# A causal convolution of four taps, moved from multiply-adds on VectorE to accumulating float32 matmuls on TensorE, in a hybrid decoder layer

## The chip, the cores and the metric

The kernel runs on one core of a Trainium2 chip. The metric is the device time of one execution in microseconds (us); lower is better. The kernel before took 1670.52 us, the median of three runs (1668.51 to 1672.82). The names of the engines are those of the profile: PE is TensorE's matmuls, PEld its weight loads, DVE is VectorE, ACT is ScalarE, POOL is GpSimd, and SP issues most of the transfers.

## The reference

One decoder layer for 1024 tokens of 1024 channels, everything in float32. A mixer (a gated delta rule of four heads of 128 channels, beside an S5 state space model of 512 channels) is followed by cross-attention to 256 memory tokens and by a SwiGLU. The part that the change touches is the way from the in-projection to the heads:

```python
def _causal_dwconv(x, w):                       # w: 4 taps for each channel
    return lax.conv_general_dilated(
        x, w[:, None, :], window_strides=(1,), padding=((CONV_WIDTH - 1, 0),),
        dimension_numbers=("NWC", "WIO", "NWC"), feature_group_count=x.shape[-1])

proj = xn @ w_in                                # xn = RMSNorm(x)
qkv = silu(_causal_dwconv(proj[..., OFF_Q:OFF_Z], conv_w))
q, k, v = three times 512 columns of qkv, as 4 heads of 128
...
mn = _rmsnorm(mem, norm_mem_g)
k = (mn @ w_xk).reshape(bsz, N_MEM, X_HEADS, X_HEAD_DIM)
v = (mn @ w_xv).reshape(bsz, N_MEM, X_HEADS, X_HEAD_DIM)
```

So each output of the convolution at token t is w0 p(t−3) + w1 p(t−2) + w2 p(t−1) + w3 p(t), channel by channel, with zeros ahead of the first token.

## The kernel before

Activations lie channel-major: 128 channels on the partitions, tokens along the free axis, in two halves of HT = 512 tokens (NT = 1024). Products that need float32 accuracy are made by `mm3` (L77 to L81): each operand is split into a high and a low part of a shorter format (fp32r), and three matmuls, high x high, low x high and high x low, accumulate in PSUM. A weight tile (`weight`) is loaded into `wraw` (two buffers), ACT copies its high part (L62, `whi`), and POOL or DVE subtracts for the low part (L63, `wlo`). A few small products are plain float32 matmuls.

The in-projection of q, k and v is twelve tiles of 128 channels, `in_tile(n)` for n = 0 to 11, twice 24 matmuls of 512 columns each. For each half DVE multiplies the PSUM tile by the row of reciprocal norms into `pre` (L477), which has four columns ahead of its tokens. Three of these are zeroed (L479, first half) or copied from the end of the first half (L481, second half). ACT then writes the first tap's product (L485), DVE adds the other three with three multiply-adds (L487), and ACT applies Silu in place (L488). `pre` has three buffers, in the pool `cv`.

For each head in turn the program makes its k and q tiles, the decays and products of keys (`dn_a`: L591 turns the keys token-major, L608 multiplies keys by keys, L626 queries by keys), its v tile, the token-major values (`dn_v`, L646) and the inverse of the chunks' triangles (`dn_b`, ending at L718). After the four heads eight chunks follow one another (`dn_seq`, L747 to L772), with the output norm and gate of each (`dn_tail`; its split is L65 and L66). In parallel the S5 part and its gate (`glu`, L902 and L904) run. Then come the operands of the output projection (`out_acts`, from L935) and the folding of memory keys into query weights (`fold_k`).

The memory tokens are normalised in `mem_prep`, and `mem_proj` makes their keys and values in 16 tiles (24 matmuls of 256 columns each). Each tile is copied by ACT from PSUM to a staging tile `mst` (L837) of the permanent pool `cp`, with one buffer, and stored to DRAM (`memD`). Later `mem_load` reads the keys and values back, into `kst` tiles of the pool `kv`.

PSUM has eight banks of 512 float32 columns. `mm` tiles come from the pool `pm` (three banks); `aux` tiles at this place come from `p5`, which has one bank.

The program is written in the order above, but a scheduler reorders the instructions of each engine by a model of times, within what buffers and data allow. Each engine, and SP's queue of transfers, then runs its instructions in that fixed order. A pool occupies its space from where it is opened to where it is closed: a pool that is opened in the space of a closed one gives its tiles only when the last users of the closed one are done. The pool `kv` is opened on the right side after `seq.close()`, which gives up the buffers of the delta rule.

Of the kernel before, what the change touches and what calls it, by code (L numbers as in the profile page):

```python
# [28 lines left out]
# columns of the packed constants: identity, upper triangle, diagonals and masks of 16-blocks  # L29
# [16 lines left out]
class Kernel:  # L46
# [12 lines left out]
    def split(self, src, hi, lo, scale=None, eng=None):  # L59
        """hi + lo = src * scale exactly, each with few enough bits for one pass of the tensor engine."""  # L60
        if scale is None:
            self.a.activation(out=hi, in_=src, func=AF.Copy)  # L62
            return (eng or self.v).tensor_tensor(out=lo, in0=src, in1=hi.bitcast(F32), op=ALU.subtract)  # L63
        else:
            self.a.activation(out=hi, in_=src, func=AF.Copy, scale=scale)  # L65
            self.v.scalar_tensor_tensor(out=lo, in0=src, scalar=scale, in1=hi.bitcast(F32), op0=ALU.mult, op1=ALU.subtract)  # L66

    def weight(self, src, n, m, eng=None):
        """src: DRAM [128, n, m] -> (hi, lo) [128, n, m]."""
        raw = self.wp.tile([P, n, m], F32, name="wraw", bufs=2)  # L70
        self.load(raw, src)
        hi = self.wp.tile([P, n, m], F32R, name="whi")
        lo = self.wp.tile([P, n, m], F32R, name="wlo")
        self.split(raw, hi, lo, None, eng)
        return hi, lo
# [24 lines left out]
    def exact_exp(self, out, x, n, r, w):  # L100
        """exp(x) to float32 accuracy, 0 below the normal range; n, r, w: scratch."""
# [14 lines left out]
    def colsum(self, ps, srcs):  # L116
        """ps[:, 64 i] = sums over the partitions of srcs[i] [128, 128]; -> view [128, n]."""
        for i, xs in enumerate(srcs):
            for j, x in enumerate(xs):
                self.lastc = self.te.matmul(ps[:, 64 * i:64 * i + 64], x, self.ones, start=(j == 0), stop=(j == len(xs) - 1))  # L120
        return ps[:, 0:64 * len(srcs)].rearrange("p (t n) -> p t n", n=64)[:, :, 0]

    def rstd(self, acc, nt, name, psum=None):
        """acc [128 ch, nt*128]: squares summed over channel tiles -> rstd [128 tok, nt]."""
# [10 lines left out]
    def rowbc(self, rs, nt, out, psum=None):  # L135
        """rs [128 tok, nt] -> out [128, nt*128], every row the same."""
# [13 lines left out]
    def s5_setup(self, tp):  # L150
# [24 lines left out]
        # cos and sin: quadrant reduction and series  # L175
# [35 lines left out]
        # a^p, p = 0..8  # L211
# [11 lines left out]
        # (a - 1) / (a_re + i a_im)  # L223
# [15 lines left out]
        # a^p co, as rows [re|im][p][pair (e s)]  # L239
# [10 lines left out]
        # discretised input matrices, block diagonal over the pair  # L250
# [13 lines left out]
        # unit phasors of a^(8 (n + 1))  # L264
# [23 lines left out]
        # impulse responses behind seven zero blocks  # L288
# [9 lines left out]
    def s5_pre(self, S, m, sp):  # L298
        """Matrices of eight groups (four pairs) for chunks of 8 tokens."""
# [8 lines left out]
        # (re, -im) of a^p c  # L308
# [18 lines left out]
        # impulse responses within a chunk  # L327
# [10 lines left out]
        # input matrices, rows (7 - j, c)  # L338
# [11 lines left out]
    def s5_toeplitz(self, S):  # L350
        """TT[(7 - j', c'), g, (j, c)] = response at lag j - j' of c to c'."""
# [3 lines left out]
    def s5_in(self, b, sp):  # L355
        """Inputs of the states of four groups at the chunks."""
# [18 lines left out]
    def s5_out(self, b, sp, M, U4, Tt, Pv):  # L375
        """States by a real scan in rotated axes, and the outputs."""
# [44 lines left out]
    def x_prep(self, h, cv, first=None):  # L421
        """Split gain * x for a token half; statistics for its RMSNorm."""
# [28 lines left out]
    def proj_tile(self, src, xh, xl, w=None, ps=None):  # L451
        """One 128-column tile of a projection for a token half, channel-major in PSUM."""
# [6 lines left out]
    def in_tile(self, n, cv, w=None, px=None, stats=False):  # L459
        """A tile of the in-projection, both halves; n: 0..11 q|k|v through the causal convolution, 12..15 u."""  # L460
# [3 lines left out]
        last = None  # L464
        for h in range(2):
# [4 lines left out]
            if n >= 12:  # L470
# [4 lines left out]
                continue  # L475
            pre = cv.tile([P, 4 + HT], F32, name="pre", bufs=3)
            v.tensor_tensor(out=pre[:, 4:], in0=ps, in1=rb, op=ALU.mult)  # L477
            if h == 0:
                v.memset(pre[:, 1:4], 0.0)  # L479
            else:  # L480
                v.tensor_copy(out=pre[:, 1:4], in_=last[:, HT + 1:HT + 4])  # L481
            last = pre
            cw = lambda i: self.convw[:, n, i:i + 1]
            acc = out[:, h * HT:(h + 1) * HT]
            self.a.activation(out=acc, in_=pre[:, 1:1 + HT], func=AF.Copy, scale=cw(0))  # L485
            for i in (1, 2, 3):
                v.scalar_tensor_tensor(out=acc, in0=pre[:, 1 + i:1 + i + HT], scalar=cw(i), in1=acc, op0=ALU.mult, op1=ALU.add)  # L487
            self.a.activation(out=acc, in_=acc, func=AF.Silu)  # L488
# [6 lines left out]
    def zab(self, cv):  # L495
        """z, a, b token-major: two blocks of 260 columns."""
        ab = cv.tile([P, 8, 8], F32, name="ab", bufs=1)
        for blk in (1, 0):
            ws = [self.weight(self.I["w_z"][blk, q], 4, 260) for q in range(2)]
            for c in range(8):  # L500
# [12 lines left out]
                zt = cv.tile([P, 260], F32, name="zt", bufs=2)  # L513
# [7 lines left out]
    def gates(self, ab, cv):  # L521
        """g = -exp(a_log) softplus(a + dt_bias), beta = sigmoid(b), and the cumulated g of each chunk."""
# [5 lines left out]
        # softplus(x) = max(x, 0) + log1p(exp(-|x|)); log1p(e) = 2 atanh(e / (2 + e))  # L528
# [33 lines left out]
    def dn_a(self, hd, q, k, dp, dx):  # L562
        """A head in eight chunks of 128 tokens: decays, products of keys and queries."""
# [12 lines left out]
        # decays  # L576
# [11 lines left out]
        # keys token-major  # L588
# [16 lines left out]
        # -L, strictly lower  # L605
# [7 lines left out]
        # its diagonal 16-blocks, every row on all 16 partitions of its block  # L613
# [9 lines left out]
        # queries against keys [s, c], s <= c  # L623
# [7 lines left out]
        # eps of the output norm, scaled by the norm of the query  # L631
# [9 lines left out]
    def dn_v(self, hd, vT, b1, dp):  # L641
        """Values token-major."""
# [8 lines left out]
    def dn_b(self, hd, L, R, dp):  # L651
        """The inverse of each chunk's triangle."""
# [10 lines left out]
        # N = (I + L)^-T: 16-blocks by substitution  # L663
# [12 lines left out]
        # doubled to 32, 64 and 128; M = N^T; only every second block of columns changes  # L676
# [46 lines left out]
    def slot(self, name):  # L723
        """The next of the buffers of a name in the space that the heads have left."""
# [4 lines left out]
    def dn_seq(self, c, dq):  # L729
        """The state across chunks, and the outputs of a chunk."""  # L730
# [44 lines left out]
    def dn_tail(self, c, po, dq, xs):  # L775
        """Norm and gate of a chunk's outputs, channel-major and split."""
# [22 lines left out]
    def mem_prep(self, cv):  # L799
        """RMSNorm of the memory tokens, split."""  # L800
        T = lambda n, i: self.tmp.tile([P, HT], F32, name=n, bufs=i)
        two = lambda t: t.rearrange("p (k t) -> p k t", k=2)
        raws = [T(n, 2) for n in ("res", "res", "fsg")] + [cv.tile([P, 4 + HT], F32, name="pre", bufs=3)[:, 4:]]
# [24 lines left out]
    def mem_proj(self, mem, w, dst):  # L828
        """Keys or values of the memory, channel-major."""
        mh, ml = mem  # L830
        for m in range(KD):
# [4 lines left out]
            t = self.cp.tile([P, NMEM], F32, name="mst")  # L836
# [11 lines left out]
    def fold_k(self, kv, K, m):  # L848
        """Query weights against the keys of each head: scores = x AD."""
# [11 lines left out]
    def fold_v(self, kv, V, hd, c):  # L861
        """Values of a head against the rows of the output weights."""
# [47 lines left out]
    def resid(self, w, order, xs, accs):  # L910
        """hT += w^T x for (tile, half) in order; squares summed on the way."""
# [10 lines left out]
    def out_acts(self, xs, tp):  # L922
        """Right sides of the seven products of the output projection."""
# [7 lines left out]
        def diff(x, y, k, name):  # L931
            """x - y of two operands in two parts."""
# [20 lines left out]
    def out_pair(self, mp, X, accs):  # L953
        """hT = x + w_out^T (outputs of the mixer) for two tiles and both halves, by seven products."""
# [63 lines left out]
    def scores(self, c, xs, rs, qp, between):  # L1018
        """Softmax of two heads for a half. The rows go without the factor of the RMSNorm: the softmax scale carries it."""
# [29 lines left out]
    def probs(self, p, pT, c, n):  # L1049
        """Probabilities of a head with a tile of the memory on the partitions, split."""  # L1050
# [20 lines left out]
    def ffn_prep2(self, acc, x0, xp, kx, T4):  # L1071
        """Right sides of the seven products, from the normalised rows of both halves."""
# [50 lines left out]
    def raw_pair(self, f, xp, gp):  # L1123
        """Gate and up columns of two tiles."""
# [8 lines left out]
    def ff_pair(self, f, raws, X, xp, gp, order, prep=None):  # L1133
        """Gate and up of two tiles and both halves, 2 x 2 blocks by seven products (Winograd's form of Strassen's)."""
# [25 lines left out]
        def add(u, o, x, y):  # L1160
            """have[o] = have[x] + have[y]; outputs are (tile, half)."""
# [54 lines left out]
    def down_acts(self, c, raw=None):  # L1216
        """Right sides of a chunk of four rows of the down projection, from DRAM: products 1, 2, 3 and 7, and the sums of the others."""
# [47 lines left out]
    def down_weights(self, c, mp, pool, n=2):  # L1265
        """Left sides of the seven products for two output tiles."""
# [17 lines left out]
    def down_products(self, c, mp, X, W):  # L1284
        """Seven products; those that enter several outputs gather in Q."""
# [24 lines left out]
    def out_rows(self, m, o):  # L1310
        """Output tile m for a token range within a half."""
# [3 lines left out]
    def down_last(self):  # L1315
        """Operands of the last two rows of the down projection."""
# [16 lines left out]
    def ff_down(self, m, o, acts, ws):  # L1333
        """The last two rows of the down projection into output tile m, for a token range."""
# [6 lines left out]
    def final(self, o, rs):  # L1341
        """Last RMSNorm of a token range."""
# [36 lines left out]
    def emit(self, ctx):  # L1379
# [73 lines left out]
        with psum("ps6", 1) as self.p6, psum("pds", 1) as self.ps, psum("pdo", 2) as self.po:  # L1453
# [19 lines left out]
            self.mem_proj(mem, "w_xk", self.memD[0])  # L1473
            self.mem_proj(mem, "w_xv", self.memD[1])
# [114 lines left out]
def _layout(x, mem, norm_mix_g, w_in, conv_w, dn_a_log, dn_dt_bias, dn_norm_g,  # L1589
# [11 lines left out]
    # channels of the S5 part: within a tile of eight groups, (channel, group)  # L1601
# [46 lines left out]
```

## Time and profile before

| | |
|---|---|
| median of three runs | 1670.52 us (1668.51 to 1672.82) |
| span of the profiled execution | 1669.7 us, 20638 instructions |
| busy ACT, POOL | 646.7 us (39%), 703.0 us (42%) |
| mean granted TensorE clock | 0.935 of full speed |
| bytes moved | 208.63 MB, 125 GB/s on the mean |
| last head's key products (L608) | at 370.3 us |
| last `pre` multiply (L477) and last Silu (L488) start | 378.9 and 388.9 us |
| staging copies of the memory (L837) | 16, from 392.9 to 578.8 us |

The profile is of one execution; times in it count from its first instruction. "Busy" is the time in which an engine ran an instruction. Matmuls are pipelined, so their records overlap; the price of one is read from the distance between the starts of neighbours. A wait is written as the waiting engine, tile and line, then "<-" and what released it.

### The profile page before, as it was taken

To read this page: it belongs to the slowest core of one execution; us is meant where nothing else is said; L and a number is where in the kernel's file an instruction comes from. 1 tells how busy PE (TensorE), PEld (TensorE's weight loads), DVE (VectorE), ACT (ScalarE), POOL (GpSimd) and SP (SyncE) were. 2 spreads that over 40 slices of the span, in tenths; PEclk is the share of its full clock that TensorE was granted. 3 is DMA by queue.
4 is the path that set the end of the run, shared out by engine and by line. 5 is a ranking of instruction groups with operands and counts; after the bars stand their busy time and mean duration, and the time that the engine had idled before them with its cause. 6 is when DMAs were issued, how large, how long until landed. Compare 5 with 4: busy or idle time off the path is not lost. (4 is left out here: it accounts for less than half of the span.)

```text
span 1669.7 us, 20638 instructions
## 1 busy us (share of the span) xinstructions
PE 1496.9 (90%) x7302; PEld 1245.7 (75%) x7302; DVE 1262.7 (76%) x2176; ACT 646.7 (39%) x1164; POOL 703.0 (42%) x507
## 2 busy tenths in 40 slices
PE   6887978988878988999999889999999997889985
PEld 4776767877878876878888668888888885677764
DVE  8968987976689898875547895555555559999995
ACT  5222443342345653454533333333333334433322
POOL 6074432313444566610011554333333357556554
PEclk8998989989688989999999889999999999999997
DMA  6256534345686453235424212322222134233202
GB/s 215 79 163 199 175 92 115 94 123 177 222 297 234 145 171 120 89 127 175 153 89 151 88 57 85 105 89 88 88 77 82 51 122 181 89 101 101 89 0 101
DMA packets 123894, 208.63 MB, mean 125 GB/s; under 512 B 10224, under 2 KB 69520, under 8 KB 121232
## 3 DMA queue, kind: packets, MB, share of 16 engines
q1 hardware_dynamic: 123792, 207.33, 38.6%
q8 instruction: 57, 0.93, 0.2%
q14 instruction: 45, 0.37, 0.1%
HBM read 151.34 MB, written 58.05 MB: 125 GB/s over the span
## 5 line engine op out<-in xcount | busy, mean ns | idle before, releaser
L62 ACT ACTIVATE whi<-wraw 128x1024 fp32r<-128x1024 f32 (+2 forms) x176 | 154.0, 881 | 284.4 <-PE aux L81 77.6
L63 POOL TENSOR_TENSOR wlo<-wraw,whi 128x1024 fp32r<-128x1024 f32 x48 | 121.6, 2533 | 203.5 <-ACT whi L62 191.0
L79 PE MATMUL mm<-AH,whi 128*128 128x512 f32 x436 | 175.6, 403 | 1.1 <-ACT whi L62 1.1
L81 PE MATMUL mm<-AH,wlo 128*128 128x512 f32 x420 | 168.3, 401 | 0.0
L80 PE MATMUL mm<-AL,whi 128*128 128x512 f32 x396 | 158.4, 400 | 0.0
L147 POOL TENSOR_TENSOR acc<-acc,sq 128x512 f32<-128x512 f32 (+1 forms) x41 | 55.4, 1351 | 213.0 <-ACT sq L146 212.2
L63 DVE TENSOR_TENSOR wlo<-wraw,whi 128x1024 fp32r<-128x1024 f32 (+2 forms) x76 | 95.8, 1263 | 32.1 <-ACT whi L62 32.1
L1174 POOL TENSOR_TENSOR sg<-sg,ca 128x512 f32<-128x512 f32 x44 | 67.0, 1522 | 113.0 <-DVE sg L1167 82.0
L79 PEld LDWEIGHTS mm<-AH,whi 128*128 128x128 f32 x436 | 83.6, 192 | 19.6 <-ACT whi L62 1.8
L80 PE MATMUL aux<-AL,whi 128*128 128x512 f32 x228 | 92.3, 405 | 6.0 <-POOL AL L63 3.7
L81 PEld LDWEIGHTS mm<-AH,wlo 128*128 128x128 f32 x420 | 80.4, 191 | 18.2 <-issue 0.4
L80 PEld LDWEIGHTS mm<-AL,whi 128*128 128x128 f32 x396 | 76.4, 193 | 16.5
L487 DVE SCALAR_TENSOR_TENSOR it<-pre,convw,it 128x512 f32<-128x512 f32 x72 | 74.8, 1039 | 6.5 <-ACT it L485 5.7
L79 PE MATMUL aux<-AH,whi 128*128 128x512 f32 x188 | 75.1, 400 | 3.3 <-ACT whi L62 2.6
L62 ACT ACTIVATE wlo<-graw 128x512 fp32r<-128x512 f32 x66 | 41.6, 630 | 79.5 <-PE aux L81 57.1
L81 PE MATMUL aux<-AH,wlo 128*128 128x512 f32 x172 | 69.3, 403 | 0.0
L81 PE MATMUL aux<-AH,whi 128*128 128x512 f32 x148 | 58.6, 396 | 0.0
L80 PEld LDWEIGHTS aux<-AL,whi 128*128 128x128 f32 x228 | 44.1, 193 | 17.7 <-POOL AL L63 5.3
L79 PE MATMUL aux<-AH,wlo 128*128 128x512 f32 x132 | 53.9, 408 | 3.2 <-DVE sq L1167 3.2
L80 PE MATMUL aux<-AL,wlo 128*128 128x512 f32 x132 | 53.7, 406 | 0.0
L79 PEld LDWEIGHTS aux<-AH,whi 128*128 128x128 f32 x188 | 36.0, 192 | 12.5 <-ACT whi L62 2.8
L1172 ACT ACTIVATE ca<-ca 128x512 f32<-128x512 f32 x44 | 27.8, 632 | 35.6 <-DVE ca L1167 34.7
(699 smaller groups left out, 4745.3 us busy)
## 6 DMA issues: line engine op xcount, KB each, us to landing
graw<-in_w_up SPq DMA_DIRECT2D x22, 512.0 KB
actD<-sg SPq DMA_DIRECT2D x44, 256.0 KB
wraw<-in_w_down SPq DMA_DIRECT2D x20, 512.0 KB
wraw<-in_w_in SPq DMA_DIRECT2D x16, 512.0 KB
d_X<-XD SPq DMA_DIRECT2D x8, 1024.0 KB
wraw<-AD SPq DMA_DIRECT2D x16, 512.0 KB
wraw<-VD SPq DMA_DIRECT2D x16, 512.0 KB
wraw<-in_w_gate SPq DMA_DIRECT2D x12, 512.0 KB
```

The costliest lines, as they stand in the source:

```text
L62: self.a.activation(out=hi, in_=src, func=AF.Copy)
L63: return (eng or self.v).tensor_tensor(out=lo, in0=src, in1=hi.bitcast(F32), op=ALU.subtract)
L79: mm(ps, wh, xh, start=first, stop=False)
L80: mm(ps, wh, xl, start=False, stop=False)
L81: mm(ps, wl, xh, start=False, stop=last)
L147: eng.tensor_tensor(out=acc, in0=acc, in1=tmp, op=ALU.add)
L487: v.scalar_tensor_tensor(out=acc, in0=pre[:, 1 + i:1 + i + HT], scalar=cw(i), in1=acc, op0=ALU.mult, op1=ALU.add)
L1172: A.activation(out=r, in_=r, func=AF.Silu)
L1174: g.tensor_tensor(out=r, in0=r, in1=sg[o], op=ALU.mult)
```

## The change

For the q, k and v tiles, ACT first makes a tile `diag` of four 128 x 128 matrices, the identity scaled by each tap's 128 values (four copies per tile). `pre` now holds both halves behind its four columns and has two buffers; POOL zeroes the three columns once. The multiply by the norms stays on DVE. When both halves are there, each half is convolved by four plain float32 matmuls that accumulate in one bank of `p5`, with `diag` as weights and `pre`, shifted by a token each, as the moving side; ACT applies Silu from PSUM into `it`.

Other tiles move as well. `zt` in `zab` takes slots of `pre`, one raw tile of `mem_prep` becomes an `it` slot, and `mem_proj` copies into `kst` (four buffers, pool `kv`) in place of `mst`. Comments are taken out, so that lines from about L490 on stand two lower.

```diff
     def in_tile(self, n, cv, w=None, px=None, stats=False):
...
-        last = None
+        if n < 12:
+            diag = cv.tile([P, 4, P], F32, name="diag")
+            for i in range(4):
+                self.a.activation(out=diag[:, i], in_=self.ident, func=AF.Copy, scale=self.convw[:, n, i:i + 1])
+            pre = cv.tile([P, 4 + NT], F32, name="pre", bufs=2)
+            self.g.memset(pre[:, 1:4], 0.0)
         for h in range(2):
...
-                continue
-            pre = cv.tile([P, 4 + HT], F32, name="pre", bufs=3)
-            v.tensor_tensor(out=pre[:, 4:], in0=ps, in1=rb, op=ALU.mult)
-            if h == 0:
-                v.memset(pre[:, 1:4], 0.0)
             else:
-                v.tensor_copy(out=pre[:, 1:4], in_=last[:, HT + 1:HT + 4])
-            last = pre
-            cw = lambda i: self.convw[:, n, i:i + 1]
-            acc = out[:, h * HT:(h + 1) * HT]
-            self.a.activation(out=acc, in_=pre[:, 1:1 + HT], func=AF.Copy, scale=cw(0))
-            for i in (1, 2, 3):
-                v.scalar_tensor_tensor(out=acc, in0=pre[:, 1 + i:1 + i + HT], scalar=cw(i), in1=acc, op0=ALU.mult, op1=ALU.add)
-            self.a.activation(out=acc, in_=acc, func=AF.Silu)
+                v.tensor_tensor(out=pre[:, 4 + h * HT:4 + (h + 1) * HT], in0=ps, in1=rb, op=ALU.mult)
+        for h in range(2 if n < 12 else 0):
+            ps = self.p5.tile([P, HT], F32, name="aux")
+            for i in range(4):
+                self.te.matmul(ps, diag[:, i], pre[:, 1 + i + h * HT:1 + i + (h + 1) * HT], start=(i == 0), stop=(i == 3))
+            self.a.activation(out=out[:, h * HT:(h + 1) * HT], in_=ps, func=AF.Silu)
...
-                zt = cv.tile([P, 260], F32, name="zt", bufs=2)
+                zt = cv.tile([P, 4 + NT], F32, name="pre", bufs=2)
...
-        raws = [T(n, 2) for n in ("res", "res", "fsg")] + [cv.tile([P, 4 + HT], F32, name="pre", bufs=3)[:, 4:]]
+        raws = [T(n, 2) for n in ("res", "res", "fsg")] + [cv.tile([P, NT], F32, name="it", bufs=5)[:, 0:HT]]
...
-    def mem_proj(self, mem, w, dst):
+    def mem_proj(self, kv, mem, w, dst):
...
-            t = self.cp.tile([P, NMEM], F32, name="mst")
+            t = kv.tile([P, HT], F32, name="kst", bufs=4)[:, 0:NMEM]
...
-            self.mem_proj(mem, "w_xk", self.memD[0])
-            self.mem_proj(mem, "w_xv", self.memD[1])
+            self.mem_proj(kv, mem, "w_xk", self.memD[0])
+            self.mem_proj(kv, mem, "w_xv", self.memD[1])
```

How the instructions then stand on an engine, at three places. First PE in the middle of the heads, where the first head's keys are turned token-major (L591 before, L589 after) amid the split matmuls of the next tile. Before:

```order
L81 MATMUL mm<-AH,wlo 128x512
L79 MATMUL mm<-AH,whi 128x512
L80 MATMUL mm<-AL,whi 128x512
L81 MATMUL mm<-AH,wlo 128x512
L591 MATMUL da<-cst,it 128x128 x8
L79 MATMUL mm<-AH,whi 128x512
```

The same place on PE after the change:

```order
L81 MATMUL mm<-AH,wlo 128x512
L79 MATMUL mm<-AH,whi 128x512
L485 MATMUL aux<-pre,diag 128x512 x4
L589 MATMUL da<-cst,it 128x128 x4
L80 MATMUL mm<-AL,whi 128x512
L81 MATMUL mm<-AH,wlo 128x512
L589 MATMUL da<-cst,it 128x128 x4
L79 MATMUL mm<-AH,whi 128x512
```

The four matmuls of a half's convolution (L485) stand as a group among another tile's split matmuls, here between the matmuls that read the first and the second half of the same k tile. The next group comes 18 rows of split matmuls later.

Second ACT at the end of the sequential chunks, with the gate's last pieces (`yr`, `AH<-yy`) and the last chunk's split (`AH<-po`). Before:

```order
L786 ACTIVATE d_R,d_sso<-po 128x128 x4
L837 ACTIVATE mst<-mm 128x256
L62 ACTIVATE whi<-wraw 128x1024
L62 ACTIVATE gwh<-yr 128x512 x2
L837 ACTIVATE mst<-mm 128x256
L902 ACT_TABLE_LOAD
L902 ACTIVATE yr<-aux,bglu 128x512
L65 ACTIVATE AH<-po,dng 128x4x128
```

ACT at this place after the change:

```order
L900 ACTIVATE yr<-aux,bglu 128x512
L65 ACTIVATE AH<-po,dng 128x4x128
L835 ACTIVATE kst<-mm 128x256 x3
L62 ACTIVATE AH<-yy 128x512
L900 ACTIVATE yr<-aux,bglu 128x512 x3
L62 ACTIVATE AH<-yy 128x512 x3
L900 ACTIVATE yr<-aux,bglu 128x512
L62 ACTIVATE whi<-wraw 128x1024
L835 ACTIVATE kst<-mm 128x256
```

The copies `mst<-mm` (L837) stood one by one between the rows of the chunks; the first copies `kst<-mm` (L835) now stand, three together, right behind the last chunk's `AH<-po`, and the others follow, each behind the split of a weight tile (`whi<-wraw`).

Third DVE at the start of the output projection's operands (L935 before, L933 after). Before, with the splits of memory keys that were read back (`kvl<-kst`):

```order
L66 SCALAR_TENSOR_TENSOR AL<-po,dng,AH 128x4x128
L935 TENSOR_TENSOR fsg<-AH 128x512 x2
L63 TENSOR_TENSOR AL<-yy,AH 128x512
L63 TENSOR_TENSOR kvl<-kst,kvh 128x512
L63 TENSOR_TENSOR wlo<-wraw,whi 128x1024
L63 TENSOR_TENSOR kvl<-kst,kvh 128x512 x3
```

DVE there after the change:

```order
L66 SCALAR_TENSOR_TENSOR AL<-po,dng,AH 128x4x128
L63 TENSOR_TENSOR AL<-yy,AH 128x512 x5
L933 TENSOR_TENSOR fsg<-AH 128x512
L63 TENSOR_TENSOR wlo<-wraw,whi 128x1024
L933 TENSOR_TENSOR res<-AH 128x512
L933 TENSOR_TENSOR fsg<-AH 128x512
```

The row `wlo<-wraw` splits the first weight tile behind those of the memory projection (`w_xqT`, whose load stands on SP behind all the loads of `w_xv`). After the change it stands behind the first row of L933 and ahead of the others, and the splits of the keys come later.

## The prediction

> **What bounds the kernel now.** I read the page's engine totals first, then a table of windows over the stages that the change touches, then what PE waits for there, then the price of single instructions in the timeline.
>
> ```profile
> PE 1496.9 (90%) x7302; PEld 1245.7 (75%) x7302; DVE 1262.7 (76%) x2176; ACT 646.7 (39%) x1164; POOL 703.0 (42%) x507
> L487 DVE SCALAR_TENSOR_TENSOR it<-pre,convw,it 128x512 f32<-128x512 f32 x72 | 74.8, 1039 | 6.5 <-ACT it L485 5.7
> ```
>
> PE is busy for 90% of the span. The convolution's multiply-adds are 74.8 us of DVE, an engine at 76%. Whether they set the end is a matter of the stage they stand in. In the table of windows the columns are the stretch, its length, then busy time and count on PE, PEld, DVE, ACT and POOL, the granted clock, the DMA share and GB/s:
>
> ```profile
> 152.50:370.30 217.80, 189.38 (x992) 158.28 (x991) 179.08 (x374) 91.64 (x171) 67.71 (x36) 0.91 0.46 129
> 370.30:448.00 77.70, 65.78 (x450) 63.08 (x449) 52.18 (x102) 23.58 (x43) 29.41 (x23) 0.79 0.59 195
> 448.00:562.00 114.00, 94.96 (x698) 91.72 (x698) 99.84 (x241) 56.41 (x145) 51.89 (x47) 0.89 0.74 244
> 562.00:645.00 83.00, 70.30 (x377) 60.53 (x376) 78.91 (x85) 45.13 (x76) 55.04 (x32) 0.90 0.46 149
> ```
>
> Stage A, 152.5 to 370.3, is the q, k and v projection of the four heads, with the convolution, up to the last head's key products. PE is busy 189.4 of 217.8 us, DVE 179.1. PE stands idle for 217.8 − 189.4 = 28.4 us, of which the waits between 150 and 400 us name 19.9 and 5.6 us behind DVE:
>
> ```profile
> PE da L646 <- DVE dn_eq L635: 19.9, 3, 8.4
> PE da L626 <- DVE d_L L611: 5.6, 1, 5.6
> ```
>
> So PE bounds the stage, and DVE's late results cost it those gaps. Stage B, to 448.0, is the last head's triangle; stage C, to 562.0, the sequential chunks, with DVE the busiest (99.8 of 114.0); stage D, to 645.0, the operands of the output projection, with DVE busy 78.9 of 83.0.
>
> What does PE's work take at full clock? The timeline shows split matmuls of 512 columns back to back, six steps from the first to the second row here:
>
> ```profile
> 187.41 0.39 PE L79 MATMUL mm<-AH,whi 128*128 128x512 f32 x1
> 188.80 0.40 PE L79 MATMUL mm<-AH,whi 128*128 128x512 f32 x1
> ```
>
> That is (188.80 − 187.41) / 6 = 0.232 us each. A lower clock stretches it: in the next rows three steps of 256 columns take 0.64 us, and a little later 0.36 us.
>
> ```profile
> 393.95 0.41 PE L80 MATMUL mm<-acc,whi 128*128 128x256 f32 x1
> 394.59 0.41 PE L80 MATMUL mm<-acc,whi 128*128 128x256 f32 x1
> ...
> 395.93 0.28 PE L79 MATMUL mm<-res,whi 128*128 128x256 f32 x1
> 396.29 0.28 PE L79 MATMUL mm<-res,whi 128*128 128x256 f32 x1
> ```
>
> So a matmul at the low clock takes 0.64 / 0.36 = 1.8 times as long. Stage A's mean clock is 0.91: if it is either full or about half, about 18% of 217.8 us, 39 us, ran slow. Some of that was idle time; of the busy part I take some 30 us, half of which, 15 us, is excess. Stage A is then 174 us of work at full clock, 15 us lost to the clock and 28.4 us of gaps: **43 us of slack**, into which added work can go without lengthening the stage.
>
> **What the change removes.** The rows by line and shape for the stage (count, busy us, mean ns, idle before and its releaser):
>
> ```profile
> L485 ACT ACTIVATE it<-pre,convw 128x512 f32<-128x512 f32 x24 | 17.4, 723 | 51.0 <-DVE pre L477 35.3 <-DVE pre L479 15.6
> L477 DVE TENSOR_TENSOR pre<-mm,rbx 128x512 f32<-128x512 f32 x24 | 16.3, 677 | 2.4 <-PE mm L81 2.4
> L488 ACT ACTIVATE it<-it 128x512 f32<-128x512 f32 x24 | 15.1, 630 | 53.4 <-DVE it L487 53.3
> L481 DVE COPY pre<-pre 128x3 f32<-128x3 f32 x12 | 4.1, 342 | 0.2
> ```
>
> DVE loses 74.8 us of multiply-adds and 4.1 of halo copies; L477 stays. ACT loses 17.4 and gains 48 scaled copies of 128 columns. A copy of that size is in the trace:
>
> ```profile
> 482.97 0.25 ACT L786 ACTIVATE d_R<-po 128x128 f32<-128x128 f32 x1
> ```
>
> 48 x 0.25 = 12 us, so ACT is left 5 us lighter. The zeroing moves to POOL, 12 small writes on an engine that is busy 67.7 of stage A's 217.8 us. I put DVE, ACT and POOL at nothing for themselves: in stage A, DVE would be busy about 179 − 74 = 105 us, far below PE. Their cover is PE's work; without it, DVE's relief would show as a gain, which is the first rival.
>
> **What it adds on PE.** 24 halves x 4 matmuls of 512 columns in plain float32. None of that width is in the trace, but narrower ones are, each a pair of records (so x16 is eight matmuls); the second row of each pair is what PE starts next:
>
> ```profile
> 254.47 2.00 PE L608 MATMUL da<-it 128*128 128x128 f32 x16
> 256.24 0.48 PE L80 MATMUL mm<-AL,whi 128*128 128x512 f32 x1
> ...
> 158.13 1.72 PE L331 MATMUL aux<-s_G,s_bb 128*32 128x128 f32 x14
> 159.78 0.50 PE L81 MATMUL mm<-AH,wlo 128*128 128x512 f32 x1
> ...
> 396.61 1.14 PE L717 MATMUL db<-d_B,d_M 64*64 64x64 f32 x16
> 397.68 0.55 PE L646 MATMUL da<-cst,it 128*128 128x128 f32 x3
> ```
>
> A record of 128 columns takes 1.77 / 16 = 0.111 us, with 32 weight columns 1.65 / 14 = 0.118, and one of 64 columns 1.07 / 16 = 0.067. So the price follows the moving columns, and a record of 512 would take 4 x 0.111 = 0.44 us, a matmul 0.88, a half 3.5, and 24 halves **84 us**. From below, a record could cost no more than the split matmul of 512 columns: 24 x 8 x 0.232 = 44.5 us. From above, all at the low clock: 1.8 x 84 = 151 us. I take 84, since 128 columns at 0.111 are already the 0.12 that a split matmul of 256 takes, twice the price per column.
>
> Where it stands: the instruction order puts 22 of the 24 halves (77 us) ahead of the last head's L608, and 5 us of other PE work besides. Stage A then holds 174 + 5 + 77 = 256 us of work at full clock. Some slack stays. The conv group waits for the 0.68 us multiply and for ACT's diagonal; the second half's group waits until Silu (0.63 us) has emptied the one bank of its pool, and everything behind it on PE waits too. In the order some twenty split matmuls (20 x 0.232 = 4.6 us) stand between, which covers that; uncovered, 24 handoffs of Silu and a wait of about the same would be 30 us. Silu in turn waits on PE, and behind it on ACT stand the weight splits that release the next tile. I keep 16 of the 43 us: stage A 272 us, **+54**. Filled whole it is 256, +38; with nothing filled 256 + 43 = 299, +81.
>
> The granted clock was 0.91 in stage A and 0.79 in stage B, where PE has more gaps. The Trainium skill, "TensorE: Matmul & The Clock Gate", Part 1 (The HAM clock gate), says that the clock halves after an idle window of some 3.4 us and comes back after as long a busy one. The rows agree in kind (1.8 times, not quite 2). By that rule a denser stage A wins back the 15 us of clock loss, and the sum above can stand at +54; without it, the 256 us would carry 256 x 15 / 174 = 22 us of loss, and with 16 us of gaps the stage would be +76. The same rule speaks against the change in stage C, which loses PE work.
>
> **Stage B, −10 (0 to −15).** In the rows of L477 and L488 (min, median and max, first and last start):
>
> ```profile
> L477 DVE TENSOR_TENSOR pre<-mm,rbx x24: 646/680/692, 163.8 to 378.9; 128x512 f32<-128x512 f32 x24
> ...
> L488 ACT ACTIVATE it<-it x24: 614/632/635, 171.5 to 388.9; 128x512 f32<-128x512 f32 x24
> ```
>
> The last Silu starts 10.0 us after the last multiply. By PE it would be some 5: the half's 3.5 us and two handoffs. The two late halves add 7, the 5 us moved ahead leave, and two tiles of the memory projection, 5 us each at the low clock (24 x 0.21), leave this stage: −5 + 7 − 5 − 10 = −13, rounded to −10 for the S5 work that fills in.
>
> **The memory projection.** This is 16 tiles of 24 matmuls of 256 columns, one staging copy each on ACT:
>
> ```profile
> L837 ACT ACTIVATE mst<-mm x16: 365/384/401, 392.9 to 578.8; 128x256 f32<-128x256 f32 x16
> L63 POOL TENSOR_TENSOR wlo<-wraw,whi x13: 2340/2414/2687, 393.0 to 540.6; 128x1024 fp32r<-128x1024 f32 x13
> ...
> ACT d_R L756 <- PE ds L755: 15.1, 4, 8.3
> ```
>
> Now it fills PE's gaps from 393 to 579. After the change the staging tile lies in a pool that opens only when the delta-rule buffers are given up, so the first copy stands on ACT behind the last chunk's `AH<-po`. Three tiles can wait in the three PSUM banks; the other 13 run as one block behind stage C, and on DVE the split of the next weights stands right behind the first row of stage D, so stage D waits for the whole block.
>
> Stage C gains: the third row is 15.1 us of ACT waiting behind memory matmuls that PE takes in order ahead of L755, and POOL loses about seven splits of 2.4 us. Against it, PE's clock falls with its load, and DVE's 99.8 us stay. **−10** (0 to −20).
>
> The block costs, per tile, 24 x 0.12 = 2.9 us of PE, or what the chain of a weight tile allows. Its links elsewhere in the trace:
>
> ```profile
> 1508.58 1.07 ACT whi L62
> 1509.71 2.50 POOL wlo L63
> 1512.23 3.53 DMA wraw<-in_w_down
> ```
>
> 1.07 + 2.50 + 3.53 = 7.1 us, over two raw buffers 3.55 per tile. 13 x 2.9 = 38 to 13 x 3.55 = 46 us; then the stored keys are read back, one more 3.5 us transfer. Some of it overlaps the last gate work on ACT. **+40** (+30 to +50).
>
> **Sum.** +54 − 10 − 10 + 40 = +74. The profiled execution's span is 1669.7 us, 0.8 below the median of the runs shown, 1670.52, and no further time lies around it that the records show. 1669.7 + 74 = **1744**.
>
> **Rivals.**
> - *Faster: PE is not charged.* Were a float32 record of 512 columns to stream in 0.232 us, the 44.5 us would fit in the 43 us of slack, and stage A would end where it does now. For it: 28.4 us of PE gaps, 25.5 of them behind DVE, which the change relieves. Against it: the 128-column record at 0.111. If the block were hidden as well (+10), the time is 1669.7 + 0 − 10 − 10 + 10 = 1660; with the block exposed, 1690. It decides at a record of about 0.28 us.
> - *The block hides* in stage D, which is bound by DVE with PE busy 70.3 of 83.0. For it: 13 x 2.9 us are not on DVE. Against it: the order on DVE and ACT. The block then costs 10: 1714.
> - *The gaps are not filled*: one bank, ACT's queue and the in-order PE keep all 43 us of slack. Stage A +81, in all 1669.7 + 101 = 1771. For it: ACT's idle 51.0 and 53.4 us before L485 and L488 show how tightly the engines already hand over. Against it: twenty matmuls between the groups.
> - *The change does not relieve DVE where it matters*: L646 waits for DVE rows that are no part of the convolution, so its 19.9 us stay even with an idle DVE; with the other slack half filled that is about 1750, inside the forecast.
>
> **How the numbers follow.** Forecast, with its neighbours from 1725 to 1762: 0.50. Block hidden, 1700 to 1725: 0.17. Gaps not filled, to 1790: 0.21. Cheap float32 with the block exposed, about 1690: 0.04. Cheap and hidden, about 1660: 0.04. Beyond 1790 (low clock throughout): 0.04. The range **1700 to 1790** holds 0.88 of these by the cases, which I count as 8 in 10 because the terms B and C are guesses within their bounds. A difference of 0.3%, 5 us, is about what a measurement of this kernel can tell from none. Faster by more: the cheap and hidden case and a little of its neighbours, 0.05; within: 0.03; slower: 0.92.
>
> **What would show it.** Right: conv records of 0.44 us, four pairs to a half, 84 us of them; stage A some 272 us long at a clock above 0.91; the memory projection's copies (L835) nearly all behind stage C, in one stretch of 36 to 50 us with DVE idle; stage C near 104 us. Wrong: records near 0.23; L835 spread as L837 was; PE still waiting tens of us at L646 and its like; a stage A near 300.

## The result and the profile after

The changed kernel takes 1736.83 us (median of four runs, 1735.27 to 1740.82) against 1669.51 us for the kernel before on the same chip (four runs, the three named above among them): a ratio of 1.0404 (95% interval 1.0387 to 1.0421), 4% slower. The forecast was 1744, in a range of 1700 to 1790.

The engine totals of the page after the change, with the groups of the convolution's matmuls and of the multiply that feeds them:

```profile
span 1734.6 us, 21015 instructions
PE 1565.6 (90%) x7494; PEld 1266.9 (73%) x7494; DVE 1158.4 (67%) x2080; ACT 640.5 (37%) x1184; POOL 700.6 (40%) x519
L485 PE MATMUL aux<-pre,diag 128*128 128x512 f32 x192 | 88.1, 598 | 0.5 <-ACT it L486 0.5
L481 DVE TENSOR_TENSOR pre<-mm,rbx 128x512 f32<-128x512 f32 x24 | 16.3, 688 | 44.3 <-PE aux L485 21.4
```

DVE lost 104 us of work and PE gained 69, and PE's share stayed at 90%. The records' mean of 598 ns is not their price, since records overlap. The timeline of PE around the first half's convolution gives that:

```profile
192.87 3.60 PE L485 MATMUL aux<-pre,diag 128*128 128x512 f32 x8
195.90 0.80 PE L79 MATMUL mm<-AH,whi 128*128 128x512 f32 x1
196.54 0.40 PE L80 MATMUL mm<-AL,whi 128*128 128x512 f32 x1
```

From the start of the eight records to the start of the second split matmul behind them are 3.67 us; less 0.23 for the one between, 3.44 / 8 = 0.43 us for a record. 24 halves are 83 us, forecast as 84.

The windows of the changed kernel are cut at the last head's key products (427.2), the end of the last triangle (485.5), just ahead of the last chunk's split (591; it starts at 592.7) and at the last memory copy (649; it starts at 648.8); the columns are as before:

```profile
152.50:427.20 274.70, 261.94 (x1239) 190.20 (x1237) 111.09 (x292) 87.11 (x197) 69.17 (x49) 0.98 0.37 106
427.20:485.50 58.30, 51.21 (x322) 44.51 (x321) 38.09 (x88) 14.63 (x27) 22.02 (x18) 0.88 0.66 210
485.50:591.00 105.50, 79.39 (x518) 72.18 (x518) 89.27 (x258) 51.48 (x134) 39.19 (x45) 0.89 0.66 219
591.00:649.00 58.00, 51.95 (x367) 48.33 (x365) 12.25 (x12) 24.57 (x40) 34.23 (x18) 0.97 0.39 125
```

Stage A is 274.7 us long, PE busy in 261.9 of them at a clock of 0.98, and DVE in 111.1. Behind the chunks stands a stretch that the kernel before did not have: 58 us with PE busy and DVE nearly idle (12.3 us). The memory's copies and stores, and the read-back of its keys, show what it is (min/median/max ns, first to last start):

```profile
L835 ACT ACTIVATE kst<-mm x16: 362/366/402, 593.3 to 648.8; 128x256 f32<-128x256 f32 x16
...
L54 SPq DMA_DIRECT2D memD<-kst x16: 319/320/449, 593.7 to 650.1; - x16
L54 SPq DMA_DIRECT2D kst<-memD x8: 320/424/432, 649.2 to 777.2; - x8
```

All sixteen copies lie between 593.3 and 648.8 us, where they were spread from 392.9 to 578.8, and the keys are read back at 649.2 us, 573.1 before. The waits of this stretch put DVE's idle time down to PE:

```profile
DVE fsg L933 <- PE mm L81: 34.9, 1, 34.9
ACT whi L62 <- DMA wraw<-in_w_xv: 19.1, 8, 4.4
POOL wlo L63 <- ACT whi L62: 13.1, 8, 3.2
```

The row that waits is the first of the output projection's operands itself; the prediction had the weight split behind it hold the stage. Its buffer, `fsg`, is one of those in which `mem_prep` left the memory's operands, so it comes free only within the last tile of the block, at 644.8 us.

Where the time came from, read as the offset to the kernel before at the same event. Two rows of the experiments below stand here too; the marks are starts in us, and `hT` is the tile to which the products of the output projection are added:

| | key products of the last head (stage A) | last chunk's split | keys read back | first write of hT by DVE (L983, L981) | span |
|---|---|---|---|---|---|
| before | 370.6 | 575.1 | 573.1 | 641.6 | 1669.7 |
| changed | 427.2 (+56.6) | 592.7 (+17.6) | 649.2 (+76.1) | 707.6 (+66.0) | 1734.6 (+64.9) |
| changed, staging back | 425.8 (+55.2) | 621.3 (+46.2) | 618.6 (+45.5) | 688.8 (+47.2) | 1718.4 (+48.7) |
| before, late staging | 374.0 (+3.4) | 550.7 (−24.4) | 597.9 (+24.8) | 655.9 (+14.3) | 1683.9 (+14.2) |

So stage A costs 56.6 us, the triangle and the chunks give 39.0 of it back, and the rest of the way takes 64.9 − 17.6 = 47.3.

### The profile page after: what moved, and what is told of

Read it like the earlier page. It is cut to its first block, busy times and chain, and to the rows that moved or that the text cites. A ratio compares the mean times of both kernels' runs of the same rounds, so it can differ in the third digit from the quotient of the medians.

```text
span 1734.6 us, 21015 instructions
## 1 busy us (share of the span) xinstructions
PE 1565.6 (90%) x7494; PEld 1266.9 (73%) x7494; DVE 1158.4 (67%) x2080; ACT 640.5 (37%) x1184; POOL 700.6 (40%) x519
## 5 line engine op out<-in xcount | busy, mean ns | idle before, releaser
L80 PEld LDWEIGHTS mm<-AL,whi 128*128 128x128 f32 x396 | 75.1, 190 | 18.4 <-issue 3.2
L485 PE MATMUL aux<-pre,diag 128*128 128x512 f32 x192 | 88.1, 598 | 0.5 <-ACT it L486 0.5
L485 PEld LDWEIGHTS aux<-pre,diag 128*128 128x128 f32 x192 | 35.5, 190 | 35.3 <-issue 32.0
L481 DVE TENSOR_TENSOR pre<-mm,rbx 128x512 f32<-128x512 f32 x24 | 16.3, 688 | 44.3 <-PE aux L485 21.4
```

The source lines that it names most:

```text
L80: mm(ps, wh, xl, start=False, stop=False)
L485: self.te.matmul(ps, diag[:, i], pre[:, 1 + i + h * HT:1 + i + (h + 1) * HT], start=(i == 0), stop=(i == 3))
```

## The experiments

**The staging tile back.** Does the memory's block, or the convolution alone, make the loss?

```diff
-            t = kv.tile([P, HT], F32, name="kst", bufs=4)[:, 0:NMEM]
+            t = self.cp.tile([P, NMEM], F32, name="mst")
```

> The change, with only the staging tile of the memory projection back in the permanent pool, so that its 16 tiles can fill gaps again. Theory: the staging tile alone costs the block of 49 us behind the chunks and gives 22 us in the chunks and about 10 in the last head's triangle, because the filler is gone from there; undone, 1736.8 - 49 + 22 to 32 = 1710 to 1720. Rival: the chunks and the triangle got shorter because DVE is relieved by the convolution, and keep that with the filler back: 1736.8 - 49 = 1688.

1721.25 us, ratio 1.0301 (1.0284 to 1.0318): 1 us above the range of the theory, and 33 above the rival, which is out. The table's third row shows it by place. Stage A keeps its +55.2. From there to the last chunk's split the kernel gains 9.0 us with the filler (the memory's matmuls that stand in PE's gaps), 39.0 without; and from there to the end hardly anything is lost (+46.2 to +48.7). The convolution is +49 us of span, the staging tile 16 more.

**The staging tile alone**, in the kernel before (with the pool handed to `mem_proj`, as in the change):

```diff
-            t = self.cp.tile([P, NMEM], F32, name="mst")
+            t = kv.tile([P, HT], F32, name="kst", bufs=4)[:, 0:NMEM]
```

> The kernel before, with only the staging tile moved to the late pool. Theory: it costs the block (49 us) and gives back what the filler took from the chunks (22 us): 1669.5 + 27 = 1696, with 1690 to 1700 allowed. Rival 1: the gain in the chunks came from the convolution: 1669.5 + 49 = 1718. Rival 2: the block hides when the stages ahead are as before: under 1675.

1685.04 us, ratio 1.0084 (1.0064 to 1.0104). Both rivals are out, and the theory's 1696 was 11 us too high. The two parts of the change add up: 14.2 here and 48.7 above, 62.9 of 64.9 us of span. By the table the late staging gives 24.4 + 3.4 = 27.8 us from stage A's end to the last chunk's split and loses 38.6 behind it. The windows of this run, cut at the table's marks and at the first difference:

```profile
152.50:374.00 221.50, 191.03 (x995) 159.18 (x996) 180.72 (x377) 92.39 (x173) 67.97 (x36) 0.91 0.45 130
374.00:550.70 176.70, 140.16 (x940) 128.51 (x938) 146.94 (x363) 75.19 (x180) 69.58 (x69) 0.87 0.60 200
550.70:593.40 42.70, 36.24 (x296) 35.23 (x297) 1.90 (x3) 16.83 (x28) 25.41 (x12) 1.00 0.50 155
```

The third row is the block by itself: 42.7 us, DVE busy 1.9.

**Two taps of four.** Is stage A bound by PE? This kernel leaves out the first two taps and half of the convolution's matmuls.

```diff
-            for i in range(4):
-                self.te.matmul(ps, diag[:, i], pre[...], start=(i == 0), stop=(i == 3))
+            for i in (2, 3):
+                self.te.matmul(ps, diag[:, i], pre[...], start=(i == 2), stop=(i == 3))
```

> The change, with two of the four taps left out of the convolution, so half of its matmuls (the output is that of two taps). Theory: PE bounds the head stage, so the 96 records of 0.43 us that go, 41 us, come off nearly whole: 1736.8 - 38 = 1699, with 1693 to 1706 allowed. Rival: the stage is held by handoffs (one PSUM bank, ACT's and POOL's queues) and only half of it shows: 1715 or more.

1703.52 us, ratio 1.0191 (1.0172 to 1.0210): 33 of the 41 us came off, inside the theory's bounds and below the rival's 1715. Stage A of this run:

```profile
152.50:392.70 240.20, 221.67 (x1129) 171.95 (x1128) 113.16 (x284) 87.67 (x195) 69.26 (x49) 0.97 0.42 118
```

It is 34.5 us shorter for 40.3 us less of busy PE; the gaps grow from 12.8 to 18.5 us.

**Other PSUM banks** for the convolution's sums:

```diff
-            ps = self.p5.tile([P, HT], F32, name="aux")
+            ps = self.pm.tile([P, HT], F32, name="mm")
```

> The change, with the convolution's sums in the three banks that the projections use, in place of the one bank of their own. Theory: that one bank costs almost nothing, since other matmuls stand between the halves: within 6 us of 1736.8, a little over if the shared banks hold up projections. Rival: the handoff over the one bank makes the stage's 12.8 us of PE gaps; up to 13 us faster, 1724.

1749.35 us, ratio 1.0469 (1.0440 to 1.0498): 12.5 us slower than the change. The rival is out, and the theory's 6 us were too few. With the three shared banks the last head's key products start at 443.6 us, 16.4 later. The window of stage A and a row of PE's waits:

```profile
152.50:443.60 291.10, 270.58 (x1249) 195.59 (x1247) 111.36 (x296) 87.61 (x196) 69.53 (x49) 0.95 0.35 100
PE mm L485 <- DVE pre L481: 8.6, 2, 6.4
```

PE waits 8.6 us there for the multiply that feeds the convolution, which it did not in the change, and the clock is 0.95 in place of 0.98. The one bank itself cost little: in the change PE waited 0.5 us for it (the row of L485 above).

**Zeroing on DVE:**

```diff
-            self.g.memset(pre[:, 1:4], 0.0)
+            v.memset(pre[:, 1:4], 0.0)
```

> The change, with the zeroing of the three columns on DVE in place of POOL. In the profile of the change POOL stands idle 74.9 us ahead of those twelve rows, 53.1 of it waiting until the convolution two tiles ago has read the buffer, with POOL rows of the heads queued behind. Theory: the stage is bound by PE (261.9 of 274.7 us), so POOL's wait is free: within 5 us of 1736.8. Rival: it holds up the heads' chain and makes the 12.8 us of PE gaps: 1724 to 1730.

1738.44 us, ratio 1.0397 (1.0370 to 1.0423): no difference to the change. POOL's long wait was free.

**Difference tiles of their own**, so that the operands of the output projection do not wait for the memory's (the second of them, `dsq`, has one buffer in place of two):

```diff
-            t = self.tmp.tile([P, HT], F32, name=name, bufs=2)
-            u = self.tmp.tile([P, HT], F32, name="sq", bufs=2)
+            t = tp.tile([P, HT], F32, name="d" + name, bufs=2)
+            u = tp.tile([P, HT], F32, name="dsq", bufs=1)
```

> The change, with the difference tiles of the output projection's operands in buffers of their own, not in those that hold the memory's operands. Theory: what keeps DVE idle through the block of memory tiles (34.9 us at L933, put down to PE's L81) is that these buffers come free only with the block's last matmul; with others DVE works through the block, and 25 to 35 us come off: 1702 to 1712. Rival, as in the prediction: the order on DVE and the shared ACT and POOL hold stage D in any case: 1730 or more.

1746.60 us, ratio 1.0453 (1.0429 to 1.0477), some 10 us slower than the change. The theory fell, though the first part of its mechanism worked: the first difference starts at 611.7 us, not at 644.8, and DVE works through the block. But the block is then longer, as the copies' row shows, and the keys are read back 22 us later:

```profile
L933 DVE TENSOR_TENSOR dres<-AH x4: 677/1738/2749, 611.7 to 656.1; 128x512 f32<-128x512 f32 x4
...
L835 ACT ACTIVATE kst<-mm x16: 360/366/403, 595.1 to 675.7; 128x256 f32<-128x256 f32 x16
...
L54 SPq DMA_DIRECT2D kst<-memD x8: 327/422/430, 671.3 to 786.7; - x8
```

The waits of this block, from 594 to 680 us, say who is late now:

```profile
ACT T L62 <- DVE dres L935: 21.1, 4, 7.4
ACT T L62 <- DVE dfsg L935: 16.5, 4, 6.1
PEld mm L81 <- POOL wlo L63: 11.5, 6, 3.7
PE mm L81 <- POOL wlo L63: 10.2, 6, 3.5
```

ACT runs its rows in their fixed order, and with the splits of the differences (`T`) among the splits of the memory's weights it waits 37.6 us for DVE, and PE for the weights behind them (10.2 us at POOL's `wlo`). DVE's early start was worth something behind the block: from the keys' read-back to the first write of hT by DVE are 44.9 us (671.3 to 716.2), 58.4 in the change. But the block ate more than that. Whether the one buffer of `dsq` has a part in ACT's wait was not tried.

**The same tiles in the kernel before, with late staging:**

> The kernel before, with the late staging tile and with difference tiles of their own, without the convolution on PE. Theory: the staging tile alone gave 27.8 us up to the last chunk and lost 41.3 up to the first difference; with the block beside DVE's work most of the loss goes: 1685 - 25 to 35 = 1650 to 1660, faster than the kernel before. Rival: stage D is bound elsewhere and the block stays: 1680 or more.

1695.84 us, ratio 1.0140 (1.0119 to 1.0160), 11 us above late staging alone: missed, the same way. Its keys are read back at 618.8 us against 597.9, the way from there to the first write of hT is 45.5 us against 58.0, and ACT waits 30.3 us of the block for the differences.

**The same tiles alone in the kernel before:**

> The kernel before, with only the difference tiles in buffers of their own. Theory: there the first difference (576.5 us) waits for little, since the last memory tile ends at about the same time (its copy starts at 578.8): 1663 to 1671. Rival: buffers alone are worth what they are worth with the late staging tile, 1645 or less.

1671.40 us, ratio 1.0000 (0.9988 to 1.0012): no difference, as expected of the control. So the two misses come from the tiles together with the block, not from the tiles alone.

**Only the values late**, in the kernel before with tiles of their own:

```diff
-            t = self.cp.tile([P, NMEM], F32, name="mst")
+            t = kv.tile([P, NMEM], F32, name="vst", bufs=2) if kv else self.cp.tile([P, NMEM], F32, name="mst")
...
-            self.mem_proj(mem, "w_xk", self.memD[0])
-            self.mem_proj(mem, "w_xv", self.memD[1])
+            self.mem_proj(None, mem, "w_xk", self.memD[0])
+            self.mem_proj(kv, mem, "w_xv", self.memD[1])
```

> The kernel before, with difference tiles of their own, and only the eight value tiles of the memory staged in the late pool (two buffers of their own, so that the keys are read back without waiting for them); the eight key tiles stay early, as filler. Theory: half the filler leaves the chunks (14 of the 28 us that the late staging gave), the keys' path is not lengthened, and the value tiles, 8 x 2.9 = 23 us of PE, lie beside DVE's 79 us: 1655 to 1665, faster than before. Rival: what was gained ahead of the last chunk is lost behind it once more, because the folds wait on the same weight buffers behind the value tiles: 1670 or more.

1679.95 us, ratio 1.0047 (1.0028 to 1.0066): the rival's time, and half of its account, since nothing was gained ahead of the last chunk's split that could be lost again (574.8 us, as before). The keys were read back at 574.6 us, as early as before, but the first weights of the fold were loaded at 589.4, behind the values', where the kernel before loads them at 529.9:

```profile
L54 SPq DMA_DIRECT2D wraw<-in_w_xqT x8: 333/333/333, 589.4 to 627.5; - x8
```

**The weights' low parts on DVE.** What sets the block's pace?

```diff
-            wh, wl = self.weight(self.I[w][m], KD, P, self.g)
+            wh, wl = self.weight(self.I[w][m], KD, P)
```

> The change, with the low part of the memory projection's weights made on DVE (1.3 us) in place of POOL (2.4 us). Everything behind the block keeps its distance from the read-back of the keys, which waits for the block's end. Theory: the block's pace is the chain of weights, load, ACT's split and POOL's split over two buffers; the shorter split takes 13 x 0.6 to 1.1 us / 1 off: 8 to 13 us, 1724 to 1729. Rival: PE sets the pace (52.0 of 58.0 us busy): within 5 us of 1736.8.

1735.65 us, ratio 1.0390 (1.0359 to 1.0422): by the time, the rival. The window from the last chunk's split to the read-back of the keys, in the change and then in this run:

```profile
592.70:649.20 56.50, 50.25 (x358) 46.89 (x356) 10.75 (x11) 23.64 (x39) 33.66 (x17) 0.97 0.40 128
585.40:647.40 62.00, 60.46 (x406) 55.66 (x405) 26.59 (x27) 30.99 (x49) 17.90 (x14) 0.97 0.40 124
```

With the memory's splits gone from POOL (17.9 us busy), PE's idle time in the window falls from 6.3 to 1.5 us, so the chain of weights had held the block by some 5 us, and without it PE sets the pace. The time does not show the 5 us. The order has changed too: the last chunk's split stands 7.3 us earlier, with 94 of the gate's matmuls behind it in place of 46, and the last head's key products start 3.2 us later (430.4). The read-back comes 1.8 us sooner.

**One pass.** Staging back, and the convolution's operands rounded to fp32r, so that each tap is one record:

```diff
-            diag = cv.tile([P, 4, P], F32, name="diag")
+            diag = cv.tile([P, 4, P], F32R, name="diag")
...
-            pre = cv.tile([P, 4 + NT], F32, name="pre", bufs=2)
-            self.g.memset(pre[:, 1:4], 0.0)
+            pre = cv.tile([P, 4 + NT], F32, name="pre", bufs=2).bitcast(F32R)
+            self.g.memset(pre[:, 1:4].bitcast(F32), 0.0)
```

> The change, with the staging tile back and the convolution's operands rounded to fp32r, so that each tap is one record in place of two longer ones (the low parts are left out). PE loses 192 x 0.43 - 96 x 0.23 = 61 us. Theory: the price of the change in the head stage is PE's time alone; 174 + 22 + 5 us of work and the 20 us of gaps that stay with two taps make the stage 221 us, as long as before: 1721 - 53 = 1668, no gain though DVE is relieved of 79 us. Rival: relieved of DVE's waits the stage sinks to its work, 201 to 210 us: 1645 to 1658.

1658.18 us, ratio 0.9928 (0.9899 to 0.9956): the only version here that is faster than the kernel before, by 0.7%, and 63 us faster than the same kernel in plain float32. The time is that of the upper end of the rival, 10 us below the theory. Its windows, stage A and from there to the last chunk's split (cut 0.6 us ahead of these two events, which are at 369.1 and 562.0):

```profile
152.50:368.50 216.00, 205.52 (x1118) 173.24 (x1118) 113.10 (x289) 84.90 (x194) 70.04 (x49) 0.97 0.46 133
368.50:561.40 192.90, 157.97 (x1171) 149.19 (x1170) 149.66 (x347) 82.67 (x189) 84.78 (x73) 0.92 0.70 226
```

Stage A is the theory's all the same: 216.0 us (221 by the theory, 201 to 210 by the rival), about as long as before (218.1), though DVE is busy for 113 us instead of 179. What the theory left out is behind it: from stage A's end to the last chunk's split are 192.9 us, where the kernel before has 204.5:

```profile
370.60:575.10 204.50, 172.69 (x1211) 164.91 (x1210) 164.26 (x361) 86.84 (x198) 90.55 (x75) 0.86 0.65 215
```

That is 11.6 us, near the 9.0 that the run with the staging back showed, though not in the same place. The last row of the last triangle (L718, L716 in the changed kernels) parts the stretch in two:

| us | last triangle | chunks, to the last split |
|---|---|---|
| before | 76.7 | 127.8 |
| changed | 58.3 | 107.2 |
| changed, staging back | 68.1 | 127.4 |
| before, late staging | 67.2 | 109.5 |
| one pass, staging back | 72.1 | 120.8 |

## Why the prediction was right

Point by point, by the prediction's own steps:

- **Price of the float32 matmul**: right. A record of 512 columns is 0.43 us (forecast 0.44), 83 us in all (84).
- **Stage A +54**: right, +56.6. PE bounds it: half the matmuls away take 34.5 us off it, and one short record per tap brings it back to the length before. It kept 12.8 us of gaps (16 forecast), but not for the reason given, and that is luck: the handoffs of the convolution's bank cost PE 0.5 us, and 10.2 are L644's wait for DVE, which the prediction had among its rivals. The clock rose from 0.91 to 0.98, so most of the 15 us of clock loss went (by the working of the prediction, 0.98 leaves an estimated 5). The rule of the Trainium skill, "TensorE: Matmul & The Clock Gate", Part 1 (The HAM clock gate), agrees with that: the denser stage won its clock back, and the +76 of a clock that stays at 0.91 did not come.
- **One bank and POOL's zeroing**: right that they cost next to nothing. PE waited 0.5 us for the bank, other banks were worse, and the zeroing made no difference.
- **Stages B and C, −20 together**: right in sign, half the size, −39.0. Each lies outside its own bounds, the triangle with −18.4 (0 to −15) and the chunks with −20.6 (0 to −20). The runs split it: 27.8 us by the late staging alone and 9.0 by the convolution alone. By the last table the late staging gives 18.3 in the chunks and 9.5 in the triangle, and the convolution 8.6 in the triangle and 0.4 in the chunks. The clock loss put against stage C did not come: over both stages the clock is 0.86 before, and 0.88 and 0.89 after. The terms were sized by the waits of one row each (15.1 us of ACT behind memory matmuls, the last Silu 10 us after the last multiply). Taking the filler away gave more than the waits put down to it.
- **The memory's block, +40**: right that it is exposed, +47.3 from the last chunk to the end. One step behind it failed: stage D was said to wait because DVE's weight split stands behind its first row. The first row itself waits, for a buffer that the memory's operands hold. Freed of that, DVE runs through the block and shortens the way behind it by 13.5 us, but the block's end comes 22.1 us later, since ACT then waits for DVE. The pace, between 2.9 us a tile by PE and 3.55 by the chain of weights, was right: of the 56.5 us to the read-back some 11 are 46 matmuls of the gate (at 0.23), and the rest is 3.5 a tile for thirteen tiles. Both bounds count: with the chain made shorter it is 3.1, and PE was busy for 60.5 of 62.0 us.
- **Sum**: 64.9 us of span for 74 forecast. The miss of 9 is the −19 of the chunks and triangle against +7 of the block and +3 of stage A. That these partly cancel is luck.
- **Rivals**: cheap float32 is out, by 0.43 us a record. The hidden block is out, by the copies' times. Unfilled gaps are out, by the 12.8 us. That DVE's relief would not reach L646 holds in part; PE's wait there fell from 19.9 to 10.2 us:

```profile
PE da L644 <- DVE dn_eq L633: 10.2, 3, 3.8
```

What stays open: why the triangle and the chunks gain 27.8 us without the filler, and how much of the 9 to 12 us of the convolution there is DVE's backlog at the last head; how these 9 to 12 us divide over the triangle and the chunks differs between the two runs. With the memory's matmuls their copies and weight splits left ACT and POOL too. One rival that nobody tried is the single buffer of `mst`. In the last triangle of the kernel before, ACT stands still for the store of the tile before:

```profile
ACT mst L837 <- DMA memD<-mst: 12.2, 2, 6.6
```

The triangle is long where this wait is (76.7 us; 77.8 with 12.1 us of it where the values alone are late; 79.3 with 13.4 where the difference tiles alone are new), and shorter with 2.8 us of it (staging back, 68.1) or none (late staging, 67.2; one pass, 72.1). A `mst` of two buffers would tell whether it is the cause. A split convolution in three passes, with the low parts kept, was not tried either.

## What to carry to other kernels

Before moving elementwise work to TensorE, compare the price of the form with the slack of the stage: here 83 us of two-record float32 matmuls met 43 us of slack, and lost, while the rounded ones, 96 records or some 22 us, won a little, with the low parts left out. Look at each tile that changes its pool: a staging buffer in a late pool turned sixteen matmul tiles from filler into a block, for 14 to 16 us of the 65. And an engine that idles beside a block is no proof that letting it work there helps: ask which rows of the other engines its work will stand among.

## What was unexpected

Filling PE's gaps with matmuls of another part seems to have had a price: with the memory's tiles gone from them, and their copies and splits from ACT and POOL, the way from the last head's key products to the last chunk's split fell from 204.5 to 176.7 us in the kernel before, at nearly the same clock (0.86 and 0.87), with PE busy for 140.2 us in place of 172.7. And giving a waiting engine its buffers made two kernels some 10 us slower; by the waits it was because a second engine, ACT, then had to wait for that engine's rows amid those of the block.
